# Two banks for the attention outputs and two for the scores, in place of one and three

## The chip, the cores and the metric

One core of a Trainium2 chip runs one decoder layer over 512 tokens of 1024 features. The metric is the device time of one execution, in microseconds. Three runs of the kernel before took 875.91, 876.02 and 873.52 us; their median is 875.91 us. TensorE multiplies and writes into PSUM; VectorE and ScalarE read PSUM; GpSimd works on the on-chip buffer alone.

## The reference

The layer normalises the tokens, projects them, and runs two mixers side by side: sparse attention with three branches (compressed keys, all keys of selected blocks, a window of 256), and a gated linear attention in chunks of 64. With 512 tokens there are eight blocks of 64 and eight are selected, so that the selected branch is plain causal attention. Then come cross attention to 256 memory tokens, a gated feed-forward part with a convolution over three tokens, and a last normalisation.

```python
h = rms_norm(x, ln_mix_g)
o_nsa = nsa_attention(q_a, kc, vc, ks, vs, kw, vw, gates, ...)   # sum of 3 gated softmax branches
o_gla = gla(q_b, k_b, v_b, r_b, alpha_b, ...)
x = x + (g_nsa * (o_nsa @ w_branch_nsa) + g_gla * (o_gla @ w_branch_gla)) @ w_out
x = x + memory_cross_attention(rms_norm(x, ln_x_g), rms_norm(mem, ln_mem_g), ...)
x = x + conv_ffn(rms_norm(x, ln_ffn_g), w_up, conv_w, conv_b, w_down)
return rms_norm(x, ln_final_g)
```

## The kernel before

Features lie on the 128 partitions and the 512 tokens along a row. Every large product is split: each float32 operand is held as a rounded part and a rest, and three matmuls (`mm3`, L160 to L162) replace one. Weights come in 141 blocks of 128x1024 in the order of their use; ScalarE makes the rounded part (L140), VectorE or GpSimd the rest (L141).

PSUM has eight banks, each of 128 partitions by 512 float32 values. The kernel deals them out by four tags (L85): `acc` has two banks, `sc` three, `pt` two, `o` one. `bank(tag)` (L87) asks for the next free bank of its tag; a bank is free again when the last reader of its tile is done. A first matmul into a bank therefore waits for the eviction of the tile that held it. `acc()` (L95) goes round a list of tags: `acc` alone in the first stages, `ALL_BANKS` (L91) in the merge, the memory projections and the output projection, and its first seven entries in the feed-forward part.

The order of the instructions on each engine is fixed when the program is built. They are emitted in the order of the code, and where one has no bank or buffer yet, later ones that have theirs are placed ahead of it. So on TensorE matmuls of later projections stand between those of the scores, and the counts of banks have a say in that order. Once built, each engine works its list in order: a waiting instruction holds all those behind it.

The stages, in order:

- Projections (`proj`). Queries, keys and values; four token tiles of a narrow projection in the banks of L368; the compressed keys through a small hidden layer.
- Sparse attention (`nsa`, L674). Two key heads by four blocks of 128 query rows, eight rounds. `nsa_scores` (L548) makes the scores of the compressed branch (one `sc` bank, L562) and of the four query heads against the selected and the window keys. In the first two row blocks both kinds share a bank (L578, L579), in the third and fourth each has its own (L581, L582 and L593, L594). VectorE evicts a bank with a fused addition and maximum (L584, L596; L564, L565 for the compressed branch). Then follow the exponentials (L612) and the scaling with the gates (L620 to L627). `nsa_values` (L630) of the round before follows in the code: it transposes the weights in `pt` banks (L650), splits them (L165, L166) and adds all products with the values in one `o` bank (L644), which ScalarE and VectorE empty (L664, L669). After that come zero to two `fill` projections (`fill_ps_acc`) of the linear attention. `nsa_scores` takes 5, 5, 9 and 9 banks in the four row blocks, `nsa_values` one `o` bank each time.
- Linear attention (`gla`, L686). Values of four token tiles (L688: two `acc` and two `sc` banks, evicted at L203), attention tiles (`gla_att`, one `sc` bank, evicted at L795), chunk states (`gla_states`, four banks, L739), outputs in two halves (`gla_out`, L813), with the branch products of the sparse attention as fills.
- Merge, memory keys and values, output projection, cross attention (`xat`, scores in `sc`, outputs in `o`), its output projection (`xo`, eight tiles, tags at L1011), and the feed-forward part in two halves with the last down-projection (L1113 on) and the last normalisation.

Of the kernel before, what the change touches and what calls it, by code (L numbers as in the profile page):

```python
# [58 lines left out]
def layer_kernel(ctx: ExitStack, tc: tile.TileContext, xT, memT, W, small, const, gfin, out, out_t, order):  # L59
# [19 lines left out]
    def s_(dtype=F32):  # L79
        return sb([P, T], dtype, "s", SB)  # L80

    def t_(dtype=F32):
        return sb([P, T], dtype, "t", TB)

    BANKS = {"acc": 2, "sc": 3, "pt": 2, "o": 1}  # L85

    def bank(tag):  # L87
        uid[0] += 1
        return psum.tile([P, T], F32, name=f"{stage[0]}_ps_{tag}_{uid[0]}", tag=tag, bufs=BANKS[tag])

    ALL_BANKS = ["acc", "sc", "pt", "sc", "acc", "pt", "sc", "o"]  # L91
    acc_tags = [["acc"]]
    acc_i = [-1]

    def acc():  # L95
        tags = acc_tags[0]
        acc_i[0] += 1
        return bank(tags[acc_i[0] % len(tags)])
# [54 lines left out]
    def take(desc):  # L153
        i = len(order)
        order.append(desc)
        convert(i + CONV_AHEAD)
        return convs.pop(i)

    def mm3(ps, w, x, first, last):
        nc.tensor.matmul(ps, w[0], x[0], start=first, stop=False)  # L160
        nc.tensor.matmul(ps, w[0], x[1], start=False, stop=False)  # L161
        nc.tensor.matmul(ps, w[1], x[0], start=False, stop=last)  # L162

    def split(h, l, src):
        nc.scalar.activation(h, src, AF.Copy)  # L165
        nc.vector.tensor_sub(l, src, h.bitcast(F32))  # L166

    def dense8(desc, xs, n=T, tag=None):
        w = take(desc)
        ps = bank(tag) if tag else acc()  # L170
        for k in range(KT):
            c = slice(k * P, (k + 1) * P)
            mm3(ps[:, :n], (w[0][:, c], w[1][:, c]), xs[k], k == 0, k == KT - 1)
        return ps
# [98 lines left out]
    ps = bank("o")  # L273
# [91 lines left out]


    V2 = [None] * 4
    pb = [bank(t) for t in ("sc", "sc", "pt", "o")]  # L368
    for b0, nk in ((0, 3), (3, 3), (6, 2)):
        w = take(("BB", b0, nk))  # L370
        for j in range(nk):
            k = b0 + j
            c = slice(j * BW, (j + 1) * BW)
            for t in range(4):
                ts = slice(t * P, (t + 1) * P)
                o = pb[t][:, :BW]
# [311 lines left out]
    pb = [bank(t) for t in ("acc", "acc", "sc", "sc")]  # L688
# [16 lines left out]
    def branch(name, xs, n):  # L705
        if n % 2 == 0:
            wbox[name] = take(("H", name, n))
        w = wbox[name]
        ps = acc()
        for k in range(4):  # L710
            c = slice(((n % 2) * 4 + k) * P, ((n % 2) * 4 + k + 1) * P)
            mm3(ps, (w[0][:, c], w[1][:, c]), xs[k], k == 0, k == 3)
        return ps
# [22 lines left out]

    def gla_states(m, kh, kl):
        es = slice(m * 256, (m + 1) * 256)
        banks = [bank("sc"), bank("sc"), bank("sc"), bank("pt")]  # L739
        incs = [banks[c // 4 * 2 + c % 2][:, (c // 2 % 2) * 256:(c // 2 % 2 + 1) * 256] for c in range(7)]  # L740
        for t in range(4):
            ts = slice(t * P, (t + 1) * P)
            for j, (k, v) in enumerate(((kh, 0), (kh, 1), (kl, 0))):
                for c in range(2 * t, min(2 * t + 2, 7)):
                    p0 = slice((c % 2) * 64, (c % 2) * 64 + 64)
                    nc.tensor.matmul(incs[c], k[p0, ts], vb[t][v][p0, es], start=j == 0, stop=j == 2)
        st = [None] * 8
        sts = [s_(), s_()]
        for c in range(7):
            pi = incs[c]  # L750
            s = sts[c // 4][:, (c % 4) * P:(c % 4 + 1) * P]
            for a in range(2):
                pa = slice(a * 64, a * 64 + 64)
                inc = pi[pa, a * P:(a + 1) * P]
                if c == 0:
                    nc.vector.tensor_copy(s[pa], inc)
                else:
                    nc.vector.scalar_tensor_tensor(s[pa], st[c][pa], dec[m][pa, c:c + 1], inc,
                                                   op0=ALU.mult, op1=ALU.add)
            st[c + 1] = s  # L760
        res = []
        for a in range(2):
            p0, p1 = slice(a * 64, a * 64 + 64), slice(64 - a * 64, 128 - a * 64)
            hl = []
            for j, w in ((0, 512), (1, 384)):
                x = s_(F32R)
                split(x[p0, :w], x[p1, :w], sts[j][p0, :w])
                hl.append(x)
            res.append(hl)
        return res  # L770
# [36 lines left out]
    def gla_out(m, a, st, q2, a2):  # L807
        hd = 2 * m + a
        es = slice(hd * P, (hd + 1) * P)
        po = t_()  # L810
        for u in range(2):

            ps = bank(("o", "sc")[u]).rearrange("p (a n) -> p a n", a=2)  # L813
            for t in (2 * u, 2 * u + 1):
                ts = slice(t % 2 * P, (t % 2 + 1) * P)
                nc.tensor.matmul(ps[:, :, ts], vb[t][0][:, es], a2[u][:, :, ts], start=True, stop=False)
                nc.tensor.matmul(ps[:, 0, ts], vb[t][1][:, es], a2[u][:, 0, ts], start=False, stop=False)
                for c in (2 * t, 2 * t + 1):
                    if c == 0:
                        continue  # L820
                    cs = slice(c % 4 * 64, (c % 4 + 1) * 64)
                    s = st[(c - 1) // 4][:, (c - 1) % 4 * P:((c - 1) % 4 + 1) * P]
                    nc.tensor.matmul(ps[:, :, cs], s, q2[u][:, :, cs], start=False, stop=c % 2 == 1)
            pu = po[:, u * 256:(u + 1) * 256]
            nc.scalar.activation(pu, ps[:, 1], AF.Copy)
            nc.vector.tensor_add(pu, ps[:, 0], pu)
        sq = t_()
        nc.scalar.activation(sq, po, AF.Square)
        return hd, po, sq
# [14 lines left out]
    ks = gla_keys(0)  # L844
    a0 = gla_att(*qk[0, 0])
    st = gla_states(0, *ks)
    fill(GLA_FILL[0])
    a1 = gla_att(*qk[0, 1])
    qk = {(1, a): gla_qk(1, a) for a in range(2)}
    fill(GLA_FILL[1])  # L850
    o = gla_out(0, 0, st[0], *a0)
    fill(GLA_FILL[2])
    gla_norm(*o)
    o = gla_out(0, 1, st[1], *a1)
    ks = gla_keys(1)
    fill(GLA_FILL[3])
    gla_norm(*o)
    a0 = gla_att(*qk[1, 0])
    st = gla_states(1, *ks)
    fill(GLA_FILL[4])  # L860
    a1 = gla_att(*qk[1, 1])
    fill(GLA_FILL[5])
    o = gla_out(1, 0, st[0], *a0)
    fill(GLA_FILL[6])
    gla_norm(*o)
    o = gla_out(1, 1, st[1], *a1)
# [16 lines left out]
    stage[0] = "mix"  # L883
    acc_tags[0] = ALL_BANKS
    mix = []
    for n in range(0, 8, 2):
        th = [merge(C_MG, n, t_), merge(C_MG, n + 1, t_)]
        for j in range(2):
            ps = branch("w_branch_gla", OG, n + j)
# [16 lines left out]
    for hd in range(4):  # L906
        ps = pk[hd] if hd < 2 else dense8(("A", "w_xkv", hd * P), memg, MEM)
# [9 lines left out]
    for n in range(8):  # L917
        xr = t_()
        nc.sync.dma_start(xr, xT[:, n, :])
        ps = dense8(("A", "w_out", n * P), mix)  # L920
# [7 lines left out]
    pb = [bank("pt"), bank("pt")]  # L928
# [75 lines left out]
    part = {}  # L1004

    def xo_k(n, ks):
        if n % 2 == 0 and n not in part:
            part["w", n] = take(("H", "w_xo", n))
        w = part["w", n - n % 2]
        if n not in part:  # L1010
            part[n] = bank(("acc", "acc", "sc", "sc", "sc", "acc", "acc", "sc")[n])  # L1011
        for k in ks:
            c = slice(((n % 2) * 4 + k) * P, ((n % 2) * 4 + k + 1) * P)
            mm3(part[n], (w[0][:, c], w[1][:, c]), xo[k], k == 0, k == 3)
# [8 lines left out]
    for n in range(4):  # L1023
        xo_k(n, (0, 1, 2))
    xat_values(3, p3)
    for n in range(8):
        xo_k(n, (3,) if n < 4 else range(4))
        xo_out(n)


    stage[0] = "up"
    acc_tags[0] = ALL_BANKS[:-1]
    sq2 = sqs[0]
# [46 lines left out]
    for n in range(8):  # L1080
        ps = acc()
# [31 lines left out]
    banks = [bank(t)[:, head] for t in ("acc", "acc", "sc", "sc")]  # L1113
# [8 lines left out]
    for h in range(2):  # L1122
        pt = bank("o")
# [5 lines left out]
    for n in range(4, 8):  # L1129
        ps = bank(("sc", "pt", "acc", "pt")[n - 4])[:, head]  # L1130
# [24 lines left out]
    for i, (h, c) in enumerate(((0, slice(0, T)), (1, slice(0, 256)), (1, slice(256, T)))):  # L1155
        ps = bank(("pt", "o", "sc")[i])[:, c]
# [141 lines left out]
```

## Time and profile before

| | |
|---|---|
| median of three runs | 875.91 us |
| profiled execution | 875.57 us |
| its span | 873.5 us |
| TensorE busy | 853.2 us, 98% |
| VectorE busy | 557.7 us, 64% |
| ScalarE busy | 419.1 us, 48% |
| GpSimd busy | 214.2 us, 25% |

Engines are named PE (TensorE matmul), PEld (its weight loads), DVE (VectorE), ACT (ScalarE), POOL (GpSimd) and SP. A tile's name begins with its stage, so `nsa_ps_sc` is a score bank of the sparse attention and `fill_ps_acc` a bank of a fill projection. L12 is line 12 of the kernel; a line can be that of a helper, such as `mm3` or `split`. Matmuls follow each other before the one ahead has ended, so that durations overlap and the distance of two starts is the pace. The profiled execution is longer than its span by what lies around the traced instructions, 2.1 us.

### The profile page before, as it was taken

What the parts mean: (1) busy time and instruction counts of PE and PEld (TensorE: products, weight loads), DVE (VectorE), ACT (ScalarE), POOL (GpSimd) and SP (SyncE); (2) the same over time, 40 slices, a digit from 0 to 9 for tenths busy, and PEclk for the clock granted to TensorE, in tenths of its full rate; (3) what the DMA queues carried; (4) which work ended last, traced back from release to release, by engine and by line L of the source; (5) the groups of instructions that cost most, each with busy time, mean ns of one, the idle gap of its engine ahead of it and who ended that gap; (6) DMA issues with size and microseconds to landing.
All of it is one profiled execution on the core that took longest, in us unless ns stands there. A gap on an engine that the chain in (4) does not pass through costs nothing.

```text
span 873.5 us, 11086 instructions
## 1 busy us (share of the span) xinstructions
PE 853.2 (98%) x4174; PEld 708.0 (81%) x4174; DVE 557.7 (64%) x908; ACT 419.1 (48%) x731; POOL 214.2 (25%) x160
## 2 busy tenths in 40 slices
PE   9999989999998999999999999999999999999996
PEld 6987777777786878898888788888888888888996
DVE  7576977998858378454487669665533465565324
ACT  7466767798445455344446535433311233334311
POOL 1373444344333314112300222111100111112121
PEclk9999999999999999999999999999999999999999
DMA  8333221002221232244341132322222223222302
GB/s 293 116 123 97 73 73 49 25 2 73 67 78 49 96 116 103 96 169 146 123 143 49 48 121 74 120 96 97 97 97 96 97 86 108 90 97 102 121 25 97
DMA packets 26406, 83.58 MB, mean 96 GB/s; under 512 B 3056, under 2 KB 5104, under 8 KB 26352
## 3 DMA queue, kind: packets, MB, share of 16 engines
q1 hardware_dynamic: 26064, 82.58, 27.2%
q8 instruction: 33, 0.54, 0.3%
q10 hardware_dynamic: 288, 0.28, 0.1%
q14 instruction: 21, 0.17, 0.1%
HBM read 80.76 MB, written 2.10 MB: 95 GB/s over the span
## 4 chain that ended last, share of the span: by engine, by line
PE 88%; DVE 7%; ACT 3%; issue 1%; POOL 1%; ACTq 0%; POOLq 0%
PE up_ps_sc L161 4%; PE up_ps_sc L160 4%; PE up_ps_sc L162 4%; PE fill_ps_acc L160 3%; PE fill_ps_acc L161 3%; PE fill_ps_acc L162 3%; PE up_ps_pt L160 3%; PE up_ps_pt L161 3%; PE up_ps_pt L162 3%; PE up_ps_acc L161 2%; PE up_ps_acc L160 2%; PE up_ps_acc L162 2%; PE nsa_ps_o L644 2%; PE down_ps_sc L162 2%; PE nsa_ps_pt L650 2%; PE down_ps_sc L161 2%
## 5 line engine op out<-in xcount | busy, mean ns | idle before, releaser
L1068 POOL TENSOR_TENSOR up_s<-up_s,up_s 128x512 f32<-128x512 f32 x22 | 35.8, 1630 | 259.6 <-ACT up_wh L140 207.7
L140 ACT ACTIVATE up_wh<-up_raw 128x1024 fp32r<-128x1024 f32 x40 | 42.5, 1062 | 64.9 <-PE up_ps_sc L161 33.0
L141 DVE TENSOR_TENSOR up_wl<-up_raw,up_wh 128x1024 fp32r<-128x1024 f32 x40 | 62.8, 1569 | 16.0 <-ACT up_wh L140 15.9
L141 POOL TENSOR_TENSOR fill_wl<-fill_raw,fill_wh 128x1024 fp32r<-128x1024 f32 x16 | 38.5, 2407 | 48.7 <-ACT fill_wh L140 46.7
L160 PE MATMUL up_ps_sc<-xo_g,up_wh 128*128 128x512 f32 x124 | 48.7, 393 | 0.0
L162 PE MATMUL up_ps_sc<-xo_g,up_wl 128*128 128x512 f32 x124 | 48.3, 389 | 0.0
L161 PE MATMUL up_ps_sc<-xo_g,up_wh 128*128 128x512 f32 x124 | 48.3, 389 | 0.0
L160 PE MATMUL up_ps_pt<-xo_g,up_wh 128*128 128x512 f32 x104 | 40.6, 390 | 0.0
L162 PE MATMUL up_ps_pt<-xo_g,up_wl 128*128 128x512 f32 x104 | 40.5, 389 | 0.0
L161 PE MATMUL up_ps_pt<-xo_g,up_wh 128*128 128x512 f32 x104 | 40.5, 389 | 0.0
L612 ACT ACTIVATE nsa_s<-nsa_s,nsa_nm 128x128 f32<-128x128 f32 (+3 forms) x64 | 34.2, 536 | 11.7 <-DVE nsa_nm L603 11.7
L160 PE MATMUL fill_ps_acc<-in_g,fill_wh 128*128 128x512 f32 x96 | 38.3, 399 | 0.2 <-DVE fill_t L529 0.2
L161 PE MATMUL fill_ps_acc<-in_g,fill_wh 128*128 128x512 f32 x96 | 38.3, 399 | 0.0
L162 PE MATMUL fill_ps_acc<-in_g,fill_wl 128*128 128x512 f32 x96 | 38.1, 396 | 0.0
L162 PE MATMUL up_ps_acc<-xo_g,up_wl 128*128 128x512 f32 x88 | 34.2, 389 | 0.0
L161 PE MATMUL up_ps_acc<-xo_g,up_wh 128*128 128x512 f32 x88 | 34.2, 389 | 0.0
L160 PE MATMUL up_ps_acc<-xo_g,up_wh 128*128 128x512 f32 x88 | 34.2, 389 | 0.0
L1064 ACT ACTIVATE up_s<-up_s 128x512 f32<-128x512 f32 x22 | 13.8, 632 | 40.2 <-DVE up_s L1062 40.2
L140 ACT ACTIVATE down_wh<-down_raw 128x1024 fp32r<-128x1024 f32 x9 | 9.5, 1061 | 39.4 <-PE down_ps_sc L161 17.5
L224 POOL TENSOR_TENSOR xo_g<-xo_g,xo_t 128x512 f32<-128x512 f32 x7 | 12.3, 1756 | 63.8 <-ACT xo_g L214 61.3
L140 ACT ACTIVATE fill_wh<-fill_raw 128x1024 fp32r<-128x1024 f32 x16 | 16.9, 1057 | 21.9 <-PE fill_ps_acc L161 14.9
L160 PEld LDWEIGHTS up_ps_sc<-xo_g,up_wh 128*128 128x128 f32 x124 | 23.3, 188 | 5.1 <-issue 0.2
(943 smaller groups left out, 2716.0 us busy)
## 6 DMA issues: line engine op xcount, KB each, us to landing
up_raw<-in_w SPq DMA_DIRECT2D x44, 512.0 KB, 3.2
fill_raw<-in_w SPq DMA_DIRECT2D x20, 512.0 KB, 3.2
down_raw<-in_w SPq DMA_DIRECT2D x18, 512.0 KB, 3.2
proj_raw<-in_w SPq DMA_DIRECT2D x14, 512.0 KB, 3.3
mix_raw<-in_w SPq DMA_DIRECT2D x12, 512.0 KB, 3.3
mkv_raw<-in_w SPq DMA_DIRECT2D x8, 512.0 KB, 3.2
wout_raw<-in_w SPq DMA_DIRECT2D x8, 512.0 KB, 3.4
in_s<-in_xT SPq DMA_DIRECT2D x8, 256.0 KB, 5.4
```

The lines of the kernel that those rows point to most:

```text
L140: nc.scalar.activation(wh[:, c], r[:, c], AF.Copy)
L141: lo.tensor_tensor(wl[:, c], r[:, c], wh[:, c].bitcast(F32), op=ALU.subtract)
L160: nc.tensor.matmul(ps, w[0], x[0], start=first, stop=False)
L161: nc.tensor.matmul(ps, w[0], x[1], start=False, stop=False)
L162: nc.tensor.matmul(ps, w[1], x[0], start=False, stop=last)
L224: eng.tensor_tensor(state[0], state[0], q, op=ALU.add)
L612: nc.scalar.activation(s[:, :w], s[:, :w], AF.Exp, scale=sl, bias=nm[:, c:c + 1], accum_out=sums[:, c:c + 1])
L644: nc.tensor.matmul(po, v, x, start=j == 0 and x is parts[0], stop=j == last and x is parts[-1])
L650: nc.tensor.transpose(pt[:, g * P:(g + 1) * P], srcs[g], C("ident"))
L1064: nc.scalar.activation(cv, cv, AF.Gelu_apprx_tanh)
L1068: nc.gpsimd.tensor_tensor(gm, gm, cv, op=ALU.mult)
```

## The change

The tag `sc` gets two banks and `o` two. The lists of tags that named three score banks, or one output bank, follow: the round of `ALL_BANKS`, the four banks of the narrow projection, the third bank of the chunk states, the second half of the linear-attention output, and the fifth tile of the cross attention's output projection. Other lists stay as they are, the last down-projection's among them.

```diff
-    BANKS = {"acc": 2, "sc": 3, "pt": 2, "o": 1}
+    BANKS = {"acc": 2, "sc": 2, "pt": 2, "o": 2}
...
-    ALL_BANKS = ["acc", "sc", "pt", "sc", "acc", "pt", "sc", "o"]
+    ALL_BANKS = ["acc", "sc", "pt", "o", "acc", "sc", "pt", "o"]
...
-    pb = [bank(t) for t in ("sc", "sc", "pt", "o")]
+    pb = [bank(t) for t in ("sc", "pt", "o", "o")]
...
-        banks = [bank("sc"), bank("sc"), bank("sc"), bank("pt")]
+        banks = [bank("sc"), bank("sc"), bank("o"), bank("pt")]
...
-            ps = bank(("o", "sc")[u]).rearrange("p (a n) -> p a n", a=2)
+            ps = bank("o").rearrange("p (a n) -> p a n", a=2)
...
-            part[n] = bank(("acc", "acc", "sc", "sc", "sc", "acc", "acc", "sc")[n])
+            part[n] = bank(("acc", "acc", "sc", "sc", "o", "acc", "acc", "sc")[n])
```

## Rows read from the trace of the kernel before

**Rows 1.** From the page of the profile: busy time of each engine with its share of the span and its count of instructions, and the line of the slices (40 equal ones) that gives TensorE's granted clock in tenths of full speed.

```profile
PE 853.2 (98%) x4174; PEld 708.0 (81%) x4174; DVE 557.7 (64%) x908; ACT 419.1 (48%) x731; POOL 214.2 (25%) x160
...
PEclk9999999999999999999999999999999999999999
```

**Rows 2.** Busy time by stretch: the stretch in us, its length, then the busy time and (instructions) of PE, PEld, DVE, ACT and POOL, the granted clock of TensorE, the DMA share and GB/s. The first is the attention stage, the second the linear-attention stage, the third all from there to the last down-projection.

```profile
74.00:225.00 151.00, 142.81 (x732) 112.43 (x730) 125.71 (x352) 112.24 (x275) 62.58 (x53) 0.99 0.14 47
...
225.00:290.00 65.00, 62.16 (x314) 50.99 (x313) 49.07 (x82) 30.56 (x51) 22.57 (x11) 1.00 0.19 65
...
290.00:820.00 530.00, 529.88 (x2440) 441.48 (x2439) 314.58 (x369) 215.33 (x308) 86.01 (x54) 1.00 0.31 106
```

**Rows 3.** The view of waits, TensorE alone: who waited, for whom, then us in total, times, longest in us.

```profile
PE nsa_ps_o L644 <- DVE nsa_t L669: 3.2, 4, 1.9
...
PE nsa_ps_o L644 <- DVE nsa_ptl L166: 1.2, 3, 0.5
PE nsa_ps_sc L562 <- DVE nsa_mx L596: 1.1, 1, 1.1
...
PE nsa_ps_sc L581 <- DVE nsa_mx L584: 0.9, 1, 0.9
```

**Rows 4.** TensorE's timeline: start and duration in us, engine, line, operation, tiles, shapes, count, and in brackets the idle time before it and what ended it.

```profile
78.41 0.60 PE L562 MATMUL nsa_ps_sc<-proj_kcmp,proj_g 128*128 128x62 f32 x4 [1.12 <-DVE nsa_mx L596]
...
111.06 0.47 PE L644 MATMUL nsa_ps_o<-nsa_pth,proj_g 128*128 128x512 f32 x1 [1.92 <-DVE nsa_t L669]
...
151.25 0.47 PE L644 MATMUL nsa_ps_o<-nsa_pth,proj_g 128*128 128x512 f32 x1 [0.84 <-DVE nsa_t L669]
...
167.09 0.47 PE L644 MATMUL nsa_ps_o<-nsa_pth,proj_g 128*128 128x512 f32 x1 [0.25 <-DVE nsa_t L669]
...
170.53 0.44 PE L581 MATMUL nsa_ps_sc<-in_pair,proj_g 128*128 128x384 f32 x1 [0.91 <-DVE nsa_mx L584]
```

**Rows 5.** Around the longest wait: the busy times of the stretch from 110 to 120 us (columns as in rows 2), and from TensorE's timeline one fill matmul before the wait and one behind it.

```profile
110.00:120.00 10.00, 8.94 (x36) 7.35 (x37) 6.17 (x19) 7.98 (x24) 1.49 (x2) 0.83 0.17 54
...
108.51 0.40 PE L160 MATMUL fill_ps_acc<-in_g,fill_wh 128*128 128x512 f32 x1
...
112.99 0.63 PE L162 MATMUL fill_ps_acc<-in_g,fill_wl 128*128 128x512 f32 x1
```

**Rows 6.** VectorE's timeline ahead of that wait, and GpSimd's at the same time.

```profile
106.72 2.48 DVE L627 TENSOR_TENSOR proj_cm<-proj_cm,nsa_cf 128x124 f32<-128x124 f32 x1
...
110.07 0.84 DVE L669 TENSOR_TENSOR nsa_t<-nsa_ps_o,nsa_t 64x256 f32<-64x256 f32 x2
...
106.63 2.43 POOL L141 TENSOR_TENSOR fill_wl<-fill_raw,fill_wh 128x1024 fp32r<-128x1024 f32 x1
```

**Rows 7.** TensorE's timeline: the two matmuls of a window score (384 columns), and the two of a selected-block score of the fourth row block (512 columns).

```profile
102.58 0.34 PE L593 MATMUL nsa_ps_sc<-in_pair,proj_g 128*128 128x384 f32 x1
102.75 0.34 PE L594 MATMUL nsa_ps_sc<-in_pair,proj_g 128*128 128x384 f32 x1
...
184.98 0.40 PE L581 MATMUL nsa_ps_sc<-in_pair,proj_g 128*128 128x512 f32 x1
185.21 0.40 PE L582 MATMUL nsa_ps_sc<-in_pair,proj_g 128*128 128x512 f32 x1
```

**Rows 8.** VectorE's timeline: evictions of scores, of 384 columns one after the other (first two rows), of 384 behind which TensorE had waited (third), and of the fourth row block.

```profile
102.95 0.55 DVE L584 CUSTOM_DVE_ANT_0 nsa_s<-nsa_ps_sc,in_cst 128x384 f32<-128x384 f32 x1
...
103.43 0.55 DVE L596 CUSTOM_DVE_ANT_0 nsa_s<-nsa_ps_sc,in_cst 128x384 f32<-128x384 f32 x1
...
169.93 0.54 DVE L584 CUSTOM_DVE_ANT_0 nsa_s<-nsa_ps_sc,in_cst 128x384 f32<-128x384 f32 x1
...
180.74 0.68 DVE L584 CUSTOM_DVE_ANT_0 nsa_s<-nsa_ps_sc,in_cst 128x512 f32<-128x512 f32 x1
...
181.35 0.55 DVE L596 CUSTOM_DVE_ANT_0 nsa_s<-nsa_ps_sc,in_cst 128x384 f32<-128x384 f32 x1
...
182.59 0.69 DVE L584 CUSTOM_DVE_ANT_0 nsa_s<-nsa_ps_sc,in_cst 128x512 f32<-128x512 f32 x1 [0.68 <-PE nsa_ps_sc L582]
```

**Rows 9.** Busy times from 90 to 200 us (columns as in rows 2); then from the timelines of VectorE and TensorE the second row block: two evictions of one bank, and the two matmuls that fill a bank.

```profile
90.00:200.00 110.00, 104.78 (x533) 83.64 (x533) 93.94 (x283) 84.60 (x214) 45.39 (x40) 0.98 0.14 48
...
92.05 0.41 DVE L584 CUSTOM_DVE_ANT_0 nsa_s<-nsa_ps_sc,in_cst 128x256 f32<-128x256 f32 x1
...
92.39 0.41 DVE L596 CUSTOM_DVE_ANT_0 nsa_s<-nsa_ps_sc,in_cst 128x256 f32<-128x256 f32 x1
...
90.65 0.39 PE L578 MATMUL nsa_ps_sc<-in_pair,proj_g 128*128 128x512 f32 x1
90.88 0.39 PE L579 MATMUL nsa_ps_sc<-in_pair,proj_g 128*128 128x512 f32 x1
```

**Rows 10.** The last down-projection, timelines of VectorE and TensorE: the eviction of the second pair of row blocks, and the first matmul of the fifth block.

```profile
825.08 1.08 DVE L1110 TENSOR_TENSOR wout_g<-down_ps_sc,wout_g 128x384 f32<-128x384 f32 x2
...
825.75 0.42 PE L160 MATMUL down_ps_sc<-up_pair,down_s 128*128 128x384 f32 x1
```

**Rows 11.** The linear-attention stage, timelines of TensorE and VectorE: the first matmul of the first attention tile, the eviction of the last value bank, and the eviction of the attention tile.

```profile
214.86 0.22 PE L791 MATMUL gla_ps_sc<-gla_g,gla_g 128*128 128x128 f32 x1
...
215.87 0.75 DVE L203 SCALAR_TENSOR_TENSOR gla_s<-gla_ps_sc,proj_rstdc,gla_s 128x512 fp32r<-128x512 f32 x1
...
223.36 0.73 DVE L795 COPY_PREDICATED gla_t<-in_cst,gla_ps_sc 128x512 f32<-128x512 uint32 x1
```

## The prediction

> **What bounds the kernel now.** I read the engine totals and the clock line first. TensorE is busy 98% of the span and its clock line stands at nine tenths or more in every slice [rows 1], so the time is its work plus its idle time. The change takes away no matmul, so only the idle time can move. Next the busy times by stage: the reader is to see that TensorE idles 151.00 - 142.81 = 8.2 us in the attention stage (74 to 225 us), 65.00 - 62.16 = 2.8 us in the linear-attention stage (225 to 290), and 530.00 - 529.88 = 0.1 us in all that follows up to 820 us [rows 2]. So the change is worth what it does to 11 us of idle time. Third, who TensorE waits for: 3.2 us in four waits are a value product (L644, tile o) held by L669, the VectorE addition that empties the single output bank. That is the largest entry, and the wait that a second output bank removes. 1.2 us more at L644 wait for L166, the split of a transposed tile, and stay. Scores (tile sc) already wait 1.1 and 0.9 us for evictions, with three banks [rows 3]. Fourth, where: the output waits stand at 111 (1.92 us), 151 and 167 us, with 0.2 us left for the fourth, the score waits at 78 and 170 [rows 4].
>
> The longest has a second price. Before it a 512-column matmul of a fill takes 0.40 us, soon after it 0.63; the granted clock of 110 to 120 us is 0.83 [rows 5], so for part of that stretch the lower level, 1.2 GHz, was granted: (1 - 0.83) x 10 = 1.7 us lost, after TensorE had stood still for 1.92 us.
>
> And its cause is not the bank alone. VectorE came late to L669 because one small multiplication, L627, took 2.48 us, beside a GpSimd subtraction of 2.43 us that began 0.09 us before it [rows 6].
>
> **The change part by part.** Nothing is computed more or less, and no DMA, weight block or queue moves; waits change, and with them the order in which the build places instructions.
>
> *Second output bank.* It removes the L669 waits, 3.2 us, and the clock loss behind the longest, 1.7 us: -4.9 us. The waiting product holds everything behind it on TensorE, mostly fill and value matmuls, so a removed wait lets these start earlier. Next late there are the splits (L166). Ends: -4.9 where all of it is kept; -(3.2 - 1.92) = -1.3 where the late VectorE instruction stops TensorE a few instructions further on and the clock falls all the same. I take -4.9, since after 111 us a run of fill matmuls stands ready.
>
> *Two score banks for three.* The stage takes 56 score banks (per key head 5, 5, 9, 9) and 8 output banks. With two banks, a bank's cycle is eviction, handover and refill, against what VectorE needs for two evictions back to back.
> Third row block (all 384 columns): eviction 0.55 [rows 8]; handover from the end of L584 at 169.93 + 0.54 = 170.47 to TensorE at 170.53, 0.06 [rows 4, 8]; refill by L593 and L594, 102.58 to 103.09, 0.51 [rows 7]. Sum 1.12, against 2 x 0.48 (102.95 to 103.43 [rows 8]) = 0.96. Lost 0.16 for each of four pairs, 0.6 us.
> Fourth block (512 and 384): 0.68 + 0.06 + 0.63 (184.98 to 185.61 [rows 7]) = 1.37, against 0.61 (180.74 to 181.35) + 0.48 = 1.09 [rows 8]; 0.28 x 4 = 1.1 us.
> Second block, one bank for both kinds: 0.34 + 0.41 + 0.06 + 0.62 = 1.43, against 4 x 0.34 = 1.36 [rows 9]: 0.1 us. The first, smaller, is put at as much.
> That is 1.9 us a key head and 3.9 us of VectorE time in all, if nothing else fills the holes. VectorE is busy 93.94 of 110 us there [rows 9], so some holes fall where it idles; and with three banks it sometimes waits for scores anyway, as 0.68 us at 182.59 [rows 8], where TensorE, not the bank, sets the pace. Ends: 0, where other work fills every hole, and +3.9, where each reaches TensorE. I take half, +2.0: the rows show runs of both kinds.
>
> A page bears on this. The Trainium skill (Perfetto Trace Analysis, Matmuls) says that independent matmul groups should rotate through different banks so that one group's eviction overlaps the next one's matmuls; by it the 56 short groups should lose more than the 8 long ones gain, which is the slower rival below. Rows 3 speak for the other side: the tag with one bank waits 3.2 us, the one with three 2.0.
>
> *The last down-projection (L1130).* Its fifth block took the free third score bank, now it needs the one emptied by the first half of L1110, done at 825.08 + 0.54 = 825.62, and it began at 825.75 [rows 10]: nothing, or 0.54 if the second half is what it gets. I take +0.2.
>
> *Linear attention.* The first attention tile (L791) began at 214.86 while both value banks were held; the second of them is freed by L203 at 215.87 + 0.75 = 216.62. One of the state banks must now wait for L795, 223.36 + 0.73 = 224.09 [rows 11], as one did before; the third comes from the output tag. Value products and fills stand beside both. Ends 0 and 216.62 - 214.86 = 1.8; I take +0.4, nearer the lower end because of that cover. The output halves (L813) get two banks as before: 0.
>
> *First projections, cross attention, the tags of the up-projection:* the rotations L91 still come back to a bank after seven or eight tiles, and TensorE idles 0.1 us in 530 there [rows 2], so full tiles of matmuls cover each eviction: 0. Without that cover, a 512-column eviction of some 0.7 us (0.68 for a 512-column score [rows 8]) would show in each; nothing uncovers it. The transposes at L1123 also get two banks; they stand between matmuls that go on, and one eviction of 0.7 is the most that this can win: 0.
>
> Sum: -4.9 + 2.0 + 0.2 + 0.4 = -2.3 us. The profiled execution took 875.57 us with a span of 873.5; it becomes 873.3 with a span of 871.2. It stood 0.3 below the median of 875.91, so I put the time to expect at 875.9 - 2.3 = 873.6 us.
>
> **The rivals.** *The whole gain.* Scores cost nothing because fills stand between them; the two small terms are covered too. Then -4.9, 871.0. If the new order spares the 1.2 us of split waits [rows 3] as well, 869.8. For it: the fills between scores. Against it: score waits exist already with three banks.
>
> *Scores starve VectorE (the slower side).* Place: the score runs of the third and fourth blocks. Every hole reaches TensorE, +3.9; a late VectorE instruction like L627 then stops TensorE at a score instead of an output, so only 1.3 of the output waits is won; another stop of that length costs another 1.7 of clock; with the +0.6 of the small terms: 3.9 - 1.3 + 1.7 + 0.6 = +4.9, 880.8. It decides once the score waits grow by more than the output waits shrink, from some 4 us where the clock loss goes, from 1 us where it stays. For it: VectorE 85% busy in 90 to 200 us [rows 9]. Against it: half the calls have fills between the scores.
> The Trainium skill (TensorE: Matmul & The Clock Gate, A second HAM failure mode: psum-queue depth-cycling) says that short idle times between groups while cycling through banks can make the clock swing. Here the trace shows one such swing, after the 1.92 us.
>
> *The wait only changes its name.* The banks are two for two, and the late instructions of VectorE hold TensorE elsewhere for as long: 0, 875.9. For it: L627 [rows 6] is no matter of banks. Against it: fills could run meanwhile.
>
> **How the numbers follow.** A measurement of this kernel can tell about 0.3%, 2.6 us, from no change: faster is below 873.3, slower above 878.5. Chances: the forecast 0.34 (its own range 871.5 to 876), the whole gain 0.22, starved 0.30, renamed 0.14. The forecast stands almost on the bound, four tenths of it below: 0.13, with 0.21 of the whole gain 0.34 for faster. Slower: 0.26 of the starved case and 0.02 of the others, 0.28. Within: 0.38. The range is 869.8 to 881.5: from the end of the whole gain to just above the starved case.
>
> **What would show it.** Right: no L644 wait for L669, clock 1.00 through 110 to 120 us, score waits of L562, L581 or L593 at 3 to 5 us in place of 2.0, TensorE's idle time in the attention stage near 7 us, the stages after 290 us unmoved. Wrong: score waits above 6 us or a second clock dip (starved); score waits of 2 us or less (the whole gain); a wait of some 2 us behind a slow small VectorE instruction under another line (renamed). The prediction also fails if the new placement brings other GpSimd subtractions beside VectorE's small instructions; no row can price that.

## The result and the profile after

The changed kernel took 883.19 us (median of four runs, 881.75 to 884.72), against 874.96 (873.52 to 876.02) for four runs of the kernel before: a ratio of 1.0102, 95% interval 1.0086 to 1.0117. It is 8.2 us slower. 873.6 was predicted, and the range ended at 881.5. Medians, here and below, are over the fast runs alone: single runs of scores_only (1214.72 us), fill_a_before (1064.74) and fill_c_after (1420.47) were far slower, at a lower granted clock. The profiled execution took 884.72 us, with a span of 882.9 against 873.5: 9.4 us to account for.

From the page of the changed kernel: busy times, and the clock by slices.

```profile
PE 858.6 (97%) x4174; PEld 712.4 (81%) x4174; DVE 553.7 (63%) x908; ACT 418.9 (47%) x731; POOL 216.6 (25%) x160
...
PEclk9999999999899999999999999999999999999999
```

Against [rows 1], the same 4174 matmuls keep TensorE busy 858.6 - 853.2 = 5.4 us longer. The remaining 9.4 - 5.4 = 4.0 us must be idle time; the gaps of TensorE's timeline, added up, give 13.1 us before and 17.1 after (gaps above 0.08 us). VectorE has less busy time than before, so it is not more work that makes the kernel slower.

The stages and eight stretches of 10 us of the changed kernel, with columns as in [rows 2]; the eighth number is the granted clock.

```profile
74.00:225.00 151.00, 141.22 (x702) 110.28 (x701) 120.18 (x344) 110.51 (x271) 59.61 (x51) 0.98 0.13 43
225.00:290.00 65.00, 60.89 (x295) 50.02 (x295) 49.15 (x81) 26.96 (x47) 21.05 (x12) 0.92 0.19 64
290.00:820.00 530.00, 529.05 (x2433) 439.75 (x2434) 313.34 (x374) 218.38 (x313) 93.15 (x55) 1.00 0.30 102
110.00:120.00 10.00, 10.00 (x48) 8.22 (x48) 6.18 (x17) 8.96 (x27) 2.03 (x3) 1.00 0.01 2
160.00:170.00 10.00, 7.15 (x40) 5.81 (x39) 9.76 (x24) 8.72 (x26) 4.80 (x5) 0.97 0.16 54
170.00:180.00 10.00, 9.95 (x43) 7.64 (x42) 8.18 (x29) 3.56 (x9) 1.85 (x2) 0.86 0.00 1
180.00:190.00 10.00, 8.05 (x38) 5.88 (x37) 7.20 (x20) 9.70 (x27) 5.71 (x5) 0.99 0.00 0
190.00:200.00 10.00, 9.93 (x49) 7.98 (x48) 8.85 (x27) 6.25 (x15) 0.79 (x3) 0.84 0.01 2
220.00:230.00 10.00, 7.64 (x43) 6.27 (x42) 8.85 (x12) 6.08 (x12) 3.28 (x3) 0.87 0.16 54
230.00:240.00 10.00, 10.00 (x46) 8.21 (x44) 8.50 (x21) 4.12 (x7) 1.40 (x1) 0.79 0.00 0
270.00:280.00 10.00, 8.26 (x38) 6.08 (x37) 9.59 (x10) 4.04 (x8) 3.34 (x3) 0.83 0.16 54
```

The stretch from 110 to 120 us, at 0.83 before [rows 5], is at 1.00, as forecast. But seven other stretches lie below 1.00, which makes four dips where there was one. Added up as the prediction did it, (1 - clock) x 10 over these seven, 8.5 us are lost to the lower clock, against 1.7 before: the 6.8 us more are enough for the 5.4 us of longer busy time. A busy time counts slow matmuls too: the attention stage looks fuller than it is, and the clock column has to be read beside it. TensorE idles 151.00 - 141.22 = 9.8 us in this stage, where near 7 was forecast, and 4.1 in the linear attention, where it was 2.8.

The waits of TensorE in the changed kernel, as in [rows 3].

```profile
PE nsa_ps_o L644 <- DVE nsa_ptl L166: 3.9, 6, 2.0
PE nsa_ps_sc L593 <- DVE proj_cm L565: 2.9, 1, 2.9
PE gla_ps_sc L746 <- DVE gla_s L203: 2.4, 1, 2.4
...
PE nsa_ps_sc L578 <- DVE nsa_mx L596: 1.2, 1, 1.2
```

The 3.2 us for L669 are gone. In their place stand three stops: 2.9 us at a score, 2.0 in the split waits (1.2 us in all before), and 2.4 at a chunk state, where no wait for L203 stood. TensorE's timeline shows them and the pace around them (before the first stop, at it, behind it; at the second; at the third).

```profile
165.39 0.40 PE L199 MATMUL gla_ps_acc<-fill_wh,in_g 128*128 128x512 f32 x1
...
168.86 0.41 PE L593 MATMUL nsa_ps_sc<-in_pair,proj_g 128*128 128x384 f32 x1 [2.85 <-DVE proj_cm L565]
...
170.28 0.63 PE L199 MATMUL gla_ps_acc<-fill_wh,in_g 128*128 128x512 f32 x1
...
189.63 0.65 PE L644 MATMUL nsa_ps_o<-nsa_ptl,proj_g 128*128 128x512 f32 x1 [1.95 <-DVE nsa_ptl L166]
...
228.33 0.77 PE L746 MATMUL gla_ps_sc<-gla_s,gla_t 64*128 64x256 f32 x2 [2.36 <-DVE gla_s L203]
...
232.06 0.63 PE L160 MATMUL fill_ps_acc<-in_g,gla_wh 128*128 128x512 f32 x1
```

A 512-column matmul takes 0.40 us ahead of the first stop and 0.63 behind it, 2.4 and 1.2 GHz as in [rows 5]. Each of the first three dips begins at one of these stops. The fourth (slow 512-column matmuls start from 276.6 to 278.1 us) follows two short stops, 0.88 us at 272 and 0.86 at 275; the kernel before has 0.88 and 0.98 at the same place and keeps its clock.

What VectorE and GpSimd did ahead of the three stops, from their timelines in the changed kernel; the last row is the same split in the kernel before, with no GpSimd work beside it.

```profile
164.34 3.72 DVE L166 TENSOR_TENSOR nsa_g<-nsa_t,nsa_g 128x128 fp32r<-128x128 f32 x2
...
168.44 0.27 DVE L565 TENSOR_TENSOR proj_cm<-nsa_ps_sc,proj_cm 128x124 f32<-128x124 f32 x1
...
164.25 2.39 POOL L141 TENSOR_TENSOR gla_wl<-fill_raw,gla_wh 128x1024 fp32r<-128x1024 f32 x1
166.60 1.31 POOL L505 TENSOR_TENSOR fill_g<-fill_g,fill_t 128x512 f32<-128x512 f32 x1
...
187.04 1.74 DVE L620 TENSOR_SCALAR nsa_s<-nsa_s,nsa_cf 128x384 f32<-128x384 f32 x3
...
188.90 1.27 DVE L166 TENSOR_TENSOR nsa_ptl<-nsa_ps_pt,nsa_pth 128x512 fp32r<-128x512 f32 x2
...
224.96 2.56 DVE L166 TENSOR_TENSOR nsa_g<-nsa_t,nsa_g 128x128 fp32r<-128x128 f32 x2 [0.16 <-ACT nsa_g L165]
227.44 0.74 DVE L203 SCALAR_TENSOR_TENSOR gla_s<-gla_ps_sc,proj_rstdc,gla_s 128x512 fp32r<-128x512 f32 x1
...
224.81 2.36 POOL L141 TENSOR_TENSOR fill_wl<-gla_raw,fill_wh 128x1024 fp32r<-128x1024 f32 x1 [10.60 <-ACT fill_wh L140]
...
193.46 0.48 DVE L166 TENSOR_TENSOR nsa_g<-nsa_t,nsa_g 128x128 fp32r<-128x128 f32 x2
```

Two of the stops have the cause of [rows 6] under another line. The split of the finished outputs (L672 calls it, the trace has it at the helper's L166) takes 0.48 us for its two instructions where GpSimd leaves it alone (the last row); here it takes 3.72 us beside L141 and L505, and the eviction L565 that the score waits for is queued behind it. At 224.96 us it takes 2.56 beside a 2.36 us L141, and L203 behind it is late. In all the nsa_g splits take 4.4 us before and 10.1 after, the L627 multiplications 4.4 and 2.2. The Trainium skill (SBUF — State Buffer, Who interferes with whom) says that a VectorE instruction with two inputs from the on-chip buffer contends with a GpSimd one that reads it; these rows agree. The middle stop has no such collision: the split stands behind scalings of 1.74 us that were not slow, and TensorE had simply run ahead.

Matched by the columns that the matmuls had worked through, the changed kernel was 2.3 us ahead where the kernel before stood at 116 us, and 2.5 at 156. It was behind by 5.6 at 188, 8.3 at 228 and 9.9 at 276, and by 9.2 to 9.8 from 320 us on. The forecast gain was there; three stops and four dips lost it and more.

### The profile page after: what moved, and what is told of

It reads as the page before. It is cut to its first block, busy times and chain, and to the rows that moved or that the text cites. A ratio compares the mean times of both kernels' runs of the same rounds, so it can differ in the third digit from the quotient of the medians.

```text
span 882.9 us, 11087 instructions
## 1 busy us (share of the span) xinstructions
PE 858.6 (97%) x4174; PEld 712.4 (81%) x4174; DVE 553.7 (63%) x908; ACT 418.9 (47%) x731; POOL 216.6 (25%) x160
## 4 chain that ended last, share of the span: by engine, by line
PE 87%; DVE 7%; ACT 4%; issue 1%; DMA 0%; POOL 0%; ACTq 0%; DVEq 0%
PE fill_ps_acc L161 3%; PE fill_ps_acc L160 3%; PE fill_ps_acc L162 3%; PE up_ps_pt L160 3%; PE up_ps_pt L162 3%; PE up_ps_pt L161 3%; PE up_ps_acc L162 2%; PE up_ps_sc L162 2%; PE up_ps_sc L161 2%; PE up_ps_acc L161 2%; PE up_ps_acc L160 2%; PE up_ps_sc L160 2%; PE nsa_ps_o L644 2%; PE nsa_ps_pt L650 2%; PE up_ps_o L162 1%; PE up_ps_o L161 1%
## 5 line engine op out<-in xcount | busy, mean ns | idle before, releaser
L1068 POOL TENSOR_TENSOR up_s<-up_s,up_s 128x512 f32<-128x512 f32 x22 | 39.0, 1777 | 256.5 <-ACT up_wh L140 204.4
L141 DVE TENSOR_TENSOR up_wl<-up_raw,up_wh 128x1024 fp32r<-128x1024 f32 x40 | 60.5, 1512 | 16.2 <-ACT up_wh L140 16.1
L141 POOL TENSOR_TENSOR fill_wl<-fill_raw,fill_wh 128x1024 fp32r<-128x1024 f32 x16 | 38.4, 2405 | 46.5 <-ACT fill_wh L140 46.5
L160 PE MATMUL up_ps_pt<-xo_g,up_wh 128*128 128x512 f32 x96 | 37.5, 390 | 0.0
L161 PE MATMUL up_ps_pt<-xo_g,up_wh 128*128 128x512 f32 x96 | 37.4, 389 | 0.0
L162 PE MATMUL up_ps_pt<-xo_g,up_wl 128*128 128x512 f32 x96 | 37.3, 389 | 0.0
L160 PE MATMUL up_ps_sc<-xo_g,up_wh 128*128 128x512 f32 x84 | 32.7, 389 | 0.0
L161 PE MATMUL up_ps_sc<-xo_g,up_wh 128*128 128x512 f32 x84 | 32.7, 389 | 0.0
L162 PE MATMUL up_ps_sc<-xo_g,up_wl 128*128 128x512 f32 x84 | 32.7, 389 | 0.0
L165 ACT ACTIVATE nsa_pth<-nsa_ps_pt 128x512 fp32r<-128x512 f32 x38 | 21.6, 591 | 14.9 <-PE nsa_ps_pt L650 13.9
L140 ACT ACTIVATE down_wh<-down_raw 128x1024 fp32r<-128x1024 f32 x9 | 9.5, 1061 | 39.4 <-PE down_ps_acc L161 13.1
L166 DVE TENSOR_TENSOR nsa_ptl<-nsa_ps_pt,nsa_pth 128x512 fp32r<-128x512 f32 x38 | 25.1, 683 | 4.5 <-ACT nsa_pth L165 4.5
```

Of the source, the lines that this page charges most:

```text
L140: nc.scalar.activation(wh[:, c], r[:, c], AF.Copy)
L141: lo.tensor_tensor(wl[:, c], r[:, c], wh[:, c].bitcast(F32), op=ALU.subtract)
L1068: nc.gpsimd.tensor_tensor(gm, gm, cv, op=ALU.mult)
```

## Experiments

**Which part does it.** In these kernels one bank gets a tag of its own, `x`, and `rot(key, tags)` deals tags out in turn, separately for each key.

*c_before*: three score banks and one output bank as before, the third under its own tag, also in the other stages' lists; a control.

```diff
-    BANKS = {"acc": 2, "sc": 3, "pt": 2, "o": 1}
+    BANKS = {"acc": 2, "sc": 2, "pt": 2, "o": 1, "x": 1}
...
-            ps = bank("sc")
+            ps = rot("s", ("sc", "sc", "x"))
```

> Control: all lists as before the change, but the third score bank has a tag of its own and is reached in a fixed rotation. If the counts of banks are what matters, this is within 2.6 us of the kernel before (about 875). If any new order of placement moves the time, it may stand several us away, and the other runs must be read against it.

Measured: 880.73 us against 873.83, ratio 1.0069 (1.0047 to 1.0091). It keeps step with the kernel before up to 190 us (0.2 us ahead at 108 and at 188 us); then an attention tile (L791) comes early, and a state waits for its eviction, in TensorE's timeline of this kernel:

```profile
225.56 0.58 PE L746 MATMUL gla_ps_x<-gla_s,gla_t 64*128 64x256 f32 x1 [2.08 <-DVE gla_t L795]
```

A dip comes with it (slow 512-column matmuls start from 227 to 231 us), and the kernel is 5.5 us behind at 228. The same counts of banks, dealt out in a slightly different way, cost 6.9 us.

*nsa_only*: the change in the sparse attention alone; the lists of the other stages keep what they had, with `x` as the third score bank, as in c_before.

```diff
-            ps = bank("sc")
+            ps = rot("s", ("sc",))
...
-        po = bank("o")
+        po = rot("o", ("o", "x"))
```

> The change in the sparse attention alone: scores on two banks, outputs on two in turn; all other lists as before. If score banks cost the time there, 5 to 7 us over the control (the 2.85 us and 1.95 us waits of the changed kernel and two clock drops of 1.7 us, less the output waits won). If the linear attention is to blame, within 1 us of the control or below it.

*scores_only*: the same, with still one bank for the outputs.

```diff
+        po = rot("o", ("o",))
```

> Scores on two banks, but the outputs still on one; all other lists as before, one bank idle in the sparse attention. If fewer score banks cost and a second output bank wins 3 to 5 us, this is 3 to 5 us slower than the sparse-attention change alone. If the second output bank wins nothing, both are equal.

*rest_only*: the changed lists in the other stages (against the changed kernel), with three score banks and one output bank in the sparse attention.

```diff
-            ps = bank("sc")
+            ps = rot("s", ("sc", "sc", "x"))
...
-        po = bank("o")
+        po = rot("o", ("o",))
```

> The change everywhere but in the sparse attention: its scores keep three banks and its outputs one. If the linear attention's bank lists cost the time, some 4 us over the control (the 2.4 us wait at the chunk states with a clock drop of 1.7 us). If the scores are to blame, within 1 us of the control.

Measured: nsa_only 886.96, 1.0143 (1.0127 to 1.0158); scores_only 886.74, 1.0127 (1.0097 to 1.0156); rest_only 884.6, 1.0114 (1.0098 to 1.0129). nsa_only has the attention stage of the changed kernel, with the same stops of 2.85 and 1.95 us. rest_only has that of the kernel before and goes wrong behind 190 us, like c_before, with 2.2 us at L746 for L795. The parts don't add up: each alone costs more than both together. Between nsa_only and scores_only the second output bank makes no difference, though one output bank had cost 3.2 us before. The waits of scores_only fit that:

```profile
PE nsa_ps_o L644 <- DVE nsa_ptl L166: 3.6, 5, 1.8
PE nsa_ps_pt L650 <- DVE nsa_ptl L166: 2.0, 1, 2.0
PE nsa_ps_sc L593 <- DVE nsa_mx L596: 1.8, 1, 1.8
```

With two score banks TensorE is held at scores and splits, and 0.5 us of waits on L669 is all that is left for a second bank to remove. That this is why the two are level is not shown: the second bank also changes the order, and c_before shows what that can cost.

**Bank counts or placement.** c_before left open whether any new order costs this much. So both kernels were built with other counts of fill projections behind the eight rounds, which reorders TensorE's list.

```diff
-NSA_FILL = (2, 1, 2, 1, 1, 2, 0, 0)
+NSA_FILL = (1, 1, 2, 1, 2, 1, 0, 0)
```

That is a; c is (2, 2, 1, 1, 1, 1, 0, 0), b is (2, 1, 1, 1, 1, 1, 1, 0), d is (1, 2, 1, 2, 1, 1, 0, 0).

> One score list of the kernel before (three score banks, one output bank) with the fill projections dealt out otherwise over the eight rounds: 1, 1, 2, 1, 2, 1, 0, 0. The work is the same, the placement another. Theory of the bank counts: 874 to 877, since the banks are those of before. Theory of the placement: 878 to 886, as the control with the renamed bank (880.7).

> The changed kernel with the same other fills (1, 1, 2, 1, 2, 1, 0, 0). Bank counts: some 8 us over its partner with three score banks. Placement: within 4 us of its partner, on either side.

> The kernel before with the fills 2, 2, 1, 1, 1, 1, 0, 0. Bank counts: 874 to 877. Placement: 878 to 886.

> The changed kernel with the fills 2, 2, 1, 1, 1, 1, 0, 0. Bank counts: some 8 us over its partner. Placement: within 4 us of its partner, on either side.

> The kernel before with the fill projections dealt out as 2, 1, 1, 1, 1, 1, 1, 0 in place of 2, 1, 2, 1, 1, 2, 0, 0. Same matmuls; another order on TensorE. Both theories: its own time may lie anywhere from 873 to 889, as the three-bank kernels with another placement did. Score waits 1.8 to 2.8 us, output waits at L669 about 3.

> The changed kernel with the same fills. Bank counts (two score banks cost more than a second output bank saves, at any placement): 4 to 15 us above fill_b_before, score waits 4 to 7 us. Placement (each new order is a draw, and the bank counts decide little): the difference to fill_b_before has no fixed sign, from -8 to +8, and a pair with the two/two kernel ahead is as likely as one behind.

> The kernel before with the fills dealt out as 1, 2, 1, 2, 1, 1, 0, 0. Both theories: from 873 to 889; score waits 1.8 to 2.8 us.

> The changed kernel with the fills 1, 2, 1, 2, 1, 1, 0, 0. Bank counts: 4 to 15 us above fill_d_before. Placement: from -8 to +8 around it, either sign.

Measured, with the pair of a later experiment (onpool) and the pair itself. Medians in us (each set of runs had the kernel before beside it, between 874.2 and 875.1), and TensorE's idle times in the timelines, added up over gaps above 0.15 us: at scores, at L644 and L650 for the output evictions (L664, L669) and for splits (L165, L166), and at states (L746). The first number of each cell has three score banks and one output bank, the second two and two.

| | time | scores | outputs | splits | states | PE busy |
|---|---|---|---|---|---|---|
| base | 874.96 / 883.19 | 2.0 / 4.7 | 3.2 / 0 | 1.5 / 3.9 | 1.1 / 3.2 | 853.2 / 858.6 |
| a | 888.62 / 891.09 | 2.4 / 4.1 | 0.5 / 0 | 9.3 / 6.3 | 3.5 / 3.2 | 858.6 / 857.1 |
| b | 885.94 / 884.68 | 3.2 / 1.9 | 2.4 / 0 | 4.0 / 7.9 | 1.9 / 2.2 | 859.6 / 857.5 |
| c | 874.82 / 889.65 | 2.8 / 5.9 | 0.5 / 0 | 3.6 / 6.1 | 1.2 / 3.2 | 851.0 / 859.1 |
| d | 882.16 / 886.28 | 3.0 / 3.7 | 0 / 0 | 5.9 / 7.9 | 3.6 / 3.2 | 855.8 / 856.8 |
| onpool | 878.38 / 884.28 | 1.8 / 7.0 | 1.9 / 0 | 6.0 / 3.0 | 1.4 / 2.8 | 852.4 / 858.5 |
| mean | 880.8 / 886.5 | 2.5 / 4.6 | 1.4 / 0 | 5.0 / 5.8 | 2.1 / 3.0 | 855.1 / 857.9 |

The idle and busy times are those of one profiled run each; in pair a that run was the fastest of the kernel with two and two (887.23 us), and below its partner's (889.09).

The pairs differ by +8.2, +2.5, -1.3, +14.8, +4.1 and +5.9 us. Their mean is +5.7, with a spread of 5.5; six of them leave a 95% interval of 5.7 +- 2.57 x 5.5 / 2.45 (Student's factor for six, and the root of six), or -0.1 to 11.5. Pair b is level, so bank counts don't cost 4 us at every placement, as that theory had it; four of six are slower by more than their runs scatter (the runs of pair a overlap too), which leans against the other theory, by which either sign is as likely, but six are few. Kernels with three and one spread over 14 us among themselves, and the kernel before stands at the low end: one of its five siblings is level with it (c), the others are 3 to 14 us slower.

The column of the output waits answers the first step of the prediction: a single output bank costs 3.2 us at one placement, 0 at another, 1.4 in the mean. In pair b one sees where the gain goes. TensorE's waits in its kernel with three and one, and then in that with two and two:

```profile
PE nsa_ps_o L644 <- DVE nsa_ptl L166: 3.0, 4, 2.0
...
PE nsa_ps_o L644 <- DVE nsa_t L669: 2.4, 2, 1.9
PE nsa_ps_sc L578 <- DVE nsa_mx L596: 2.0, 2, 1.4
```

```profile
PE nsa_ps_o L644 <- DVE nsa_ptl L166: 5.7, 8, 1.8
...
PE nsa_ps_sc L578 <- DVE nsa_mx L596: 1.2, 1, 1.2
```

L669 goes from 2.4 to nothing, and the same matmul waits 2.7 us more for the split. It is not so in every pair: the split waits grow by 2.0 to 3.9 us in four and fall by 3.0 in a and onpool.

**The collision at L672.** If the slow split makes the stops, it should help to move its subtraction from VectorE to GpSimd, in both kernels.

```diff
-            split(h[:, qs], l[:, qs], of[:, a])
+            nc.scalar.activation(h[:, qs], of[:, a], AF.Copy); nc.gpsimd.tensor_tensor(l[:, qs], of[:, a], h[:, qs].bitcast(F32), op=ALU.subtract)
```

> The same move in the kernel before: its longest wait hangs on another instruction (L627), so both theories say 872 to 877 unless the new placement moves it; placement theory 876 to 884.

> The changed kernel with one instruction moved: the subtraction that splits the attention output (L672) goes from VectorE to GpSimd, so that it can't stand beside a GpSimd subtraction on VectorE. If the 2.85 us score wait and the 2.4 us state wait come from these subtractions being held up (3.72 and 2.56 us in place of some 0.5), both waits go with their clock drops: 875 to 878. If they come from the number of score banks alone, 881 to 885.

Measured: 878.38, 1.0046 (1.0031 to 1.0061), and 884.28, 1.0113 (1.0094 to 1.0132). In the changed kernel the stop at L593 shrinks from 2.85 to 0.92 us, so the slow split made most of it. The wait for L203 shrinks from 2.36 to 0.74 us, with 1.23 for L795 behind it. But the time does not fall, and TensorE's timeline has another stop, 8 us on, where none was:

```profile
168.03 0.42 PE L593 MATMUL nsa_ps_sc<-in_pair,proj_g 128*128 128x384 f32 x1 [0.92 <-DVE proj_cm L565]
...
176.32 0.44 PE L593 MATMUL nsa_ps_sc<-in_pair,proj_g 128*128 128x384 f32 x1 [1.82 <-DVE nsa_mx L596]
```

The score waits grow to 7.0 us. The collision makes a stop, and without it the scores still stop.

**The state stage.** In four of the six kernels with two and two (base, a, c, d) the first state waits 2.35 or 2.36 us for L203, each time behind a 2.55 or 2.56 us split beside L141: both score banks hold values there. Here the fourth value bank comes from the output tag: in the changed kernel (vbank_o) and in those with the fills of d and c (vbank_d, vbank_c).

```diff
-    pb = [bank(t) for t in ("acc", "acc", "sc", "sc")]
+    pb = [bank(t) for t in ("acc", "acc", "sc", "o")]
```

> The changed kernel with one value bank of the linear attention taken from the output tag in place of the score tag (acc, acc, sc, o). If the 2.4 us wait at the chunk states comes from the two score banks being held by values and attention tile, it goes with its clock drop: 879 to 881. If it is VectorE's lateness whatever the bank, 882 to 885.

> fill_d_after (886.28 us) with the fourth value bank of the linear attention taken from the output tag. State stage as a mechanism: the 2.35 us wait of L746 for L203 goes, and with it the clock loss behind it (0.6 to 2 us): 2 to 4.5 us faster, 882 to 884. Renamed: another stop of 2 us takes its place, as at the base placement: 885.5 to 887.

> fill_c_after (889.72 us) with the same edit. State stage as a mechanism: 2 to 4.5 us faster, 885 to 888. Renamed: 889 to 890.5.

Measured: 883.39, 887.63 and 886.45 us, against 883.19, 886.28 and 889.65 without the edit: +0.2, +1.4 and -3.2. The wait for L203 goes in all three, and in all three a split wait of 2.19 us comes 22 to 25 us earlier, in vbank_c's timeline here:

```profile
208.26 0.80 PE L644 MATMUL nsa_ps_o<-nsa_ptl,proj_g 128*128 128x512 f32 x1 [2.19 <-DVE nsa_ptl L166]
...
236.09 0.61 PE L746 MATMUL gla_ps_sc<-gla_s,gla_t 64*128 64x256 f32 x3 [0.70 <-DVE gla_t L795]
```

In vbank_c it takes the place of a split wait of 2.03 us as well (at 216.30 in fill_c_after, gone here), in the other two of one of 0.7 us; vbank_c alone got faster (1.0136 of the kernel before beside it, against 1.0166).

**One pool of four.** *joint*: scores and outputs share the four banks of one tag, wherever `sc` or `o` is asked for.

```diff
-    BANKS = {"acc": 2, "sc": 2, "pt": 2, "o": 2}
+    BANKS = {"acc": 2, "so": 4, "pt": 2}
...
```

> Scores and outputs share one tag with four banks everywhere, so each takes what is free. Bank counts: scores have three or more most of the time and outputs wait less, 871 to 876. Placement: another draw, 876 to 886.

Measured: 883.1, 1.0104 (1.0087 to 1.012). Until 188 us it is 2.7 us ahead of the kernel before, with 2.5 us of score waits; then three stops of 1.14, 4.24 and 1.89 us follow, and it is 6.9 behind at 228. The longest, from its waits:

```profile
PE nsa_ps_o L644 <- ACT nsa_pth L165: 4.8, 2, 4.2
```

No version beat the kernel before; fill_c_before equals it, 1.0003 (0.9993 to 1.0013).

## Why the prediction was wrong

*The output waits: right here, and worth little in general.* No L644 waits for L669, the stretch at 110 us has its full clock, and the kernel was 2.5 us ahead at 156. At other placements the wait removed is 0 to 2.4 us, and where the split waits grow instead, its name changes: the rival that was given 0.14.

*Two score banks: right in size, partly by luck.* The step said +2.0, score waits of 3 to 5 us in place of 2.0. They are 4.7, and in the mean of six pairs they grow by 2.0 (2.5 to 4.6). The holes of 0.16 to 0.28 us between evictions are not what shows, though: most of the 4.7 is one stop of 2.85 us, from a collision that the sum had counted on the output bank's side only.

*"1.2 us more at L644 wait for L166, and stay": failed.* They became 3.9 in this pair. The table shows why that step was unsafe: 1.5 us of split waits (L165 and L166) is the lowest of the table's twelve kernels, and with other fills the same counts give 3.6 to 9.3. The prediction took this placement's luck for a property of the stage.

*The clock term, -4.9's second part: failed, and it is the largest.* It was put at -1.7, for one dip removed, with another 1.7 only in the starved rival. The dip went, and four came; TensorE's busy time rose by 5.4, which is 7.1 us off. The span was forecast to fall by 2.3 and rose by 9.4; of the 11.7 us between them the clock term makes 7.1, and the idle time 4.6 (forecast -3.2 + 2.0 + 0.2 + 0.4 = -0.6, measured +4.0). In this trace a dip follows each of the three stops of 1.95 us and more. In the mean of the six pairs the busy time rises by 2.8 us, about half the mean loss of 5.7.

*Linear attention, +0.4 between 0 and 1.8: too small.* The bank was right (a value bank freed by L203), though the first state waits for it and not the attention tile, and the waits at L746 rose by 2.1 us (1.1 to 3.2). The upper end left out that L203 itself can be late, behind a split that L141 slows.

*The down-projection and the other stages: right.* They were put at +0.2 and 0; behind 320 us the lag changes by 0.7 at most.

The rival that came nearest is *scores starve VectorE*, which was given 880.8 at 0.30. Its mark (a second dip) appeared, at score waits below its 6 us. It had the mechanism, a late small VectorE instruction that stops TensorE at a score instead of an output, but one dip where there were four, and neither the splits nor the states.

The prediction closed with the placement that no row can price, and gave it no width. c_before and the table priced it: the third score bank dealt out in another way costs 6.9 us, five other placements of the old counts 0 to 14. Much of the 8.2 us can therefore be the loss of a good placement. What the bank counts cost apart from that is not settled; -0.1 to 11.5 us is what six pairs leave.

## What to carry to other kernels

Where a build fills gaps by availability, a change in bank counts draws a new order of everything behind it; if one list of fills moves the time by 14 us, a sum of waits good to 2 us is no forecast of the total, and the range has to carry the spread. Before a wait is booked as a gain, ask what holds the same engine next: VectorE feeds both the eviction and the split here, and in four of six pairs the split waits grew. To judge such a change by its principle, time it at several placements, in pairs.

## What was not expected of the hardware

The clock fell after stops of 1.95 to 2.85 us, but not always: onpool_before has a stop of 1.92 us at an output, like the one in [rows 4], and shows no dip. Two stops of 0.9 us near 272 us were followed by a dip in the changed kernel and by none in the kernel before. fill_a_after has stops of 2.12 and 2.00 us and keeps its clock at both. Its stretches of 10 us around them, and the stops:

```profile
100.00:110.00 10.00, 7.09 (x33) 4.78 (x32) 9.40 (x26) 7.14 (x20) 4.60 (x4) 1.00 0.16 55
210.00:220.00 10.00, 8.00 (x47) 6.06 (x46) 8.02 (x11) 6.03 (x13) 4.97 (x3) 1.00 0.45 158
...
107.30 0.44 PE L593 MATMUL nsa_ps_sc<-in_pair,proj_g 128*128 128x384 f32 x1 [2.12 <-DVE nsa_mx L596]
...
216.29 0.50 PE L644 MATMUL nsa_ps_o<-nsa_ptl,proj_g 128*128 128x512 f32 x1 [2.00 <-DVE nsa_ptl L166]
```

So the length of a single stop does not decide it in these traces. The price of 1.7 us that the prediction put on a stop of some 2 us holds for some stops and not for others.
